# Attention steps in blocks of two, retention outputs turned in pairs, norm factors on weight rows, down's block 6 in seven products

## The chip, the cores and the metric

One core of a Trainium2 chip runs one program. The metric is the device time of one execution in microseconds (us). Smaller is better. The times of before are 1212.03 to 1213.17 us in three runs, median 1212.58.

## What is computed

One layer of a decoder trunk on 512 tokens of width 1024, in float32. `rmsnorm` divides each row by its root mean square and multiplies by a vector of gains.

```python
u = rmsnorm(h, g_pre_mix); proj = u @ w_in          # 1024 -> 12800 columns
yr = rmsnorm(retention(rq, rk, rv)) * silu(rg)      # 4 heads, keys of 256, values of 512
ya = dilated_attention(aq, ak, av)                  # 3 groups of 8 heads of 64, merged by softmax denominators
mixed = sigmoid(gr + b0) * (yr @ w_ret_out) + sigmoid(ga + b1) * (ya @ w_dil_out)
h = h + rmsnorm(mixed @ w_o, g_post_mix)
f = square(relu(rmsnorm(h, g_pre_mlp) @ w_up)) @ w_down   # 1024 -> 4096 -> 1024
h = h + rmsnorm(f, g_post_mlp)
gate = sigmoid(rmsnorm(h, g_pre_ple) @ w_ple_gate + b_ple_gate)
out = h + rmsnorm(gate * (p @ w_ple_in), g_post_ple)
```

In attention's group 0 a query sees up to 256 keys in two blocks of 128 tokens; groups 1 and 2 are cut into streams, and a query block of 128 sees one block of 128 keys.

## The kernel before

**Products.** Each float32 operand is split into a high and a low part, and a product is three passes (`PASSES`: high x high, high x low, low x high). One pass is a TensorE matmul of 128 rows by 128 columns that streams 512 columns; these are the full products (L234, L706, L778, L793, L1030). `acc_tile` does the passes for one token tile of 128 and `gemm` does four tiles, each in a PSUM bank from the pool `pacc` (tiles named a, four banks). All else goes through the pool `pps` (tiles b, four banks).

**Weights.** A weight unit is 256 rows by 512 columns. `plan` and `loads` list all units in order of use. `load_next` starts a load from the SP queue into a token-sized tile (t, pool `pt`, N_T = 26 buffers), and `prep_next` splits one into a tile w (N_W = 5 buffers): ScalarE makes the high part, VectorE the low part. `prep_next` is called when the last token tile has used a unit, so one unit is made for each one consumed.

**Attention as a filler.** Between the products of w_in the kernel does attention in small steps: `filler` spreads a list of steps over the next products, and `pump`, called after each three passes, takes the next when its turn comes. `attention` cuts a group into units: in group 0 four heads of one query block (two units to a block), in groups 1 and 2 all eight. A unit has three steps: `scores` (matmuls over 64 rows, which alternate between the upper and the lower 64 rows and between two banks, then VectorE adds the mask and takes the maximum, and ScalarE takes exponentials), `flip` (TensorE transposes the weights, ScalarE copies them out) and `weigh` (matmuls with the values). The list runs `weigh` of unit i - 2, `flip` of i - 1, `scores` of i. The scheduler of the language then orders the instructions of each engine, by priority and what it takes for ready.

**Retention.** `head` computes one head by a `quartet`. At its end four transposed pieces are put off with `later`, 12, 14, 16 and 18 steps on, each of four transposes into one bank.

**Quartets.** `quartet` computes a product of 2 x 2 blocks with seven block products instead of eight: named "11", 1, "12", 2, 4, 7 and "22", from sums and differences of blocks. The sums of weights are made in `add_quartet`, those of the left operand in `mix_in`, and `result` combines.

**The MLP.** 4096 columns are eight chunks of 512. Chunks 0 to 5 go through `down` in three calls (c = 0 to 2), each a quartet over two chunks, with one `up_unit` (a unit of w_up for a later chunk) behind each block product. Chunks 6 and 7 are plain products with w_down.

**Residuals.** `residual_features` adds a normed row to the residual, multiplies by the next norm's gains (g_pre, on VectorE) and puts the transposes into `vT` or `hT` off by a number of steps (`to_features`, L317). The root mean square itself is applied later.

## Time and profile before

| | |
|---|---|
| median of three runs | 1212.58 us |
| the profiled execution | 1212.39 us |
| its span, first to last instruction | 1210.6 us |
| TensorE (PE) busy | 1196.9 us, 99% |
| weight loads (PEld) busy | 989.3 us, 82% |
| VectorE (DVE) busy | 800.8 us, 66% |
| ScalarE (ACT) busy | 579.1 us, 48% |
| mean granted clock of TensorE | 0.997 |

Times below are from the profiled execution, which took 1.8 us more than its span. In the rows, L with a number is a line of the kernel; names are those of its tiles without numbers; "128x512 f32" is the shape that is read, and x with a number counts the instructions that a row merges. A matmul of a TensorE row is shown with a length of about 0.39 us though the next one starts earlier, so starts are compared, not lengths.

### The profile page before, as it was taken

Reading aid. Unit: us, or ns where it says so; the run is one execution under the profiler, and the core shown is the slowest. Engines: PE = TensorE matmul, PEld = TensorE weight load, DVE = VectorE, ACT = ScalarE, POOL = GpSimd, SP = SyncE. Lnnn points to the kernel's source line nnn. Section 1 sums busy time; section 2 is a strip of 40 time slices with the busy share of each in tenths; the row PEclk is TensorE's granted clock in tenths of the full one; section 3 lists DMA queues with packets and bytes.
Section 4 is the critical chain, followed back from the end, with each engine's and each line's share of the span. In section 5 each row is a group of like instructions: output and inputs, shape, how many; then the busy total and the mean of one; then the engine's idle time right before and its main releaser. Section 6 shows DMA issues by size and latency. Waiting matters only on the chain. (4 is left out here: it accounts for less than half of the span.)

```text
span 1210.6 us, 15131 instructions
## 1 busy us (share of the span) xinstructions
PE 1196.9 (99%) x5646; PEld 989.3 (82%) x5646; DVE 800.8 (66%) x1199; ACT 579.1 (48%) x979; POOL 61.5 (5%) x112
## 2 busy tenths in 40 slices
PE   9999999999999999999999999999999999999996
PEld 7888788888888888888888888888888888888885
DVE  6743644654577895959768467673585775975696
ACT  7334444346744563535445532454553554553362
POOL 1002001000000000000000020020000000000210
PEclk9999999999999999999999999999999999999998
DMA  9432141332241543342335472727142251254401
GB/s 345 143 113 74 41 146 56 115 129 88 88 168 67 198 154 112 131 137 84 127 109 205 137 259 99 289 85 280 36 161 73 82 189 53 87 188 177 156 1 70
DMA packets 53322, 158.87 MB, mean 131 GB/s; under 512 B 8832, under 2 KB 9088, under 8 KB 53248
## 3 DMA queue, kind: packets, MB, share of 16 engines
q1 hardware_dynamic: 39552, 131.82, 30.9%
q10 hardware_dynamic: 9600, 14.53, 3.7%
q0 software_dynamic: 4096, 11.55, 2.6%
q8 instruction: 44, 0.72, 0.2%
q14 instruction: 30, 0.25, 0.1%
HBM read 139.47 MB, written 14.68 MB: 127 GB/s over the span
## 5 line engine op out<-in xcount | busy, mean ns | idle before, releaser
L69 DVE TENSOR_TENSOR w<-t,w 128x1024 fp32r<-128x1024 f32 (+1 forms) x248 | 295.7, 1204 | 144.7 <-ACT w L66 143.4
L66 ACT ACTIVATE w<-t 128x1024 fp32r<-128x1024 f32 (+1 forms) x248 | 256.9, 1044 | 261.9 <-PE a L234 93.7
L234 PE MATMUL a<-u,w 128*128 128x512 f32 x1536 | 369.0, 395 | 1.0 <-ACT t L66 1.0
L234 PEld LDWEIGHTS a<-u,w 128*128 128x128 f32 x1536 | 284.0, 188 | 62.1 <-issue 2.3
L69 DVE TENSOR_TENSOR t<-t,t 128x1024 f32<-128x1024 f32 (+4 forms) x179 | 185.0, 1058 | 26.3 <-ACT t L66 18.5
L706 PE MATMUL b<-w,t 128*128 128x512 f32 x696 | 162.5, 390 | 0.0
L706 PEld LDWEIGHTS b<-w,t 128*128 128x128 f32 x696 | 130.7, 188 | 27.0
L1030 PE MATMUL a<-u,w 128*128 128x512 f32 x576 | 134.0, 390 | 0.0
L1030 PEld LDWEIGHTS a<-u,w 128*128 128x128 f32 x576 | 108.2, 188 | 22.4
L234 PE MATMUL a<-w,u 128*128 128x512 f32 (+1 forms) x504 | 114.3, 384 | 0.2 <-DVE w L69 0.2
L234 PE MATMUL a<-t,w 128*128 128x512 f32 x480 | 110.5, 391 | 0.0
L234 PEld LDWEIGHTS a<-w,u 128*128 128x128 f32 x504 | 91.1, 189 | 18.4 <-DVE w L69 0.5
L69 DVE TENSOR_TENSOR t<-a,t 128x512 f32<-128x512 f32 x72 | 55.7, 776 | 75.3 <-ACT t L66 52.1
L234 PEld LDWEIGHTS a<-t,w 128*128 128x128 f32 x480 | 89.8, 188 | 18.8 <-DVE t L69 0.4
L234 PE MATMUL a<-w,t 128*128 128x512 f32 x432 | 99.6, 391 | 0.0
L234 PEld LDWEIGHTS a<-w,t 128*128 128x128 f32 x432 | 80.8, 188 | 16.7
L66 ACT ACTIVATE t<-t 128x512 fp32r<-128x512 f32 (+1 forms) x55 | 42.1, 787 | 37.7 <-DVE t L69 37.7
L66 ACT ACTIVATE t<-a 80x512 f32<-80x512 f32 (+1 forms) x32 | 18.9, 591 | 69.6 <-PE a L234 64.8
L66 ACT ACTIVATE t<-s 128x256 f32<-128x256 f32 (+3 forms) x94 | 41.8, 488 | 21.2 <-DVE s L69 20.3
L66 ACT ACTIVATE s<-a 128x512 f32<-128x512 f32 x56 | 32.7, 593 | 39.0 <-PE a L234 30.1
L69 DVE TENSOR_TENSOR s<-a,t 128x512 f32<-128x512 f32 x40 | 26.4, 687 | 37.1 <-PE a L234 30.2
L66 ACT ACTIVATE t<-t,st 128x128 f32<-128x128 f32 (+1 forms) x96 | 39.8, 416 | 22.5 <-DVE st L482 19.4
(119 smaller groups left out, 1004.3 us busy)
## 6 DMA issues: line engine op xcount, KB each, us to landing
t<-in_w_in_dram SPq DMA_DIRECT2D x104, 512.0 KB
t<-in_w_down_dram SPq DMA_DIRECT2D x38, 512.0 KB
t<-in_w_up_dram SPq DMA_DIRECT2D x32, 512.0 KB
t<-in_w_ret_out_dram SPq DMA_DIRECT2D x16, 512.0 KB
t<-in_x_dram SPq DMA_DIRECT2D x8, 512.0 KB
yrd<-s ACTq DMA_DIRECT2D x16, 256.0 KB
t<-yrd SPq DMA_DIRECT2D x16, 256.0 KB
t<-in_w_o_dram SPq DMA_DIRECT2D x8, 512.0 KB
```

What stands on the lines that cost most here:

```text
L66: nc.scalar.activation(o, i, f, **kw)
L69: nc.vector.tensor_tensor(o, x, y, op=op)
L234: nc.tensor.matmul(ps, l, r, start=(k == 0 and q == 0), stop=(k == n - 1 and q == 2))
L706: nc.tensor.matmul(ps[t], f(k, i, t), w[:, j, k2], start=(first and k == 0 and n == 0), stop=(k == 3 and n == 2), skip_group_check=not first)
L1030: nc.tensor.matmul(state["ps"][t], w[:, i, k2, t * P:(t + 1) * P], vT[:, x, k], start=(k == 0 and n == 0), stop=(k == 7 and n == 2))
```

## The change

- Attention: units are taken two at a time. A step does `products` of two units, then their `weights` (what was `scores` is cut in these two), or two `flip`s, or two `weigh`s. The number of steps is halved.
- Retention: two transposed pieces are put off together (at 12 and 16), eight transposes in a row into two banks.
- Norm factors: g_pre_mlp and g_pre_ple are no longer multiplied into the residual's rows. They stand in the small tile `cols`, and `divide` multiplies them into the weight rows of w_up and w_ple_gate while it splits these, in two halves. The transposes read the residual itself.
- Buffers: six weight tiles, 24 token-sized tiles.
- The MLP: chunk 6 is also computed by `down`, as a quartet over the halves of one chunk (nk = 1). `gaps` says how many units of w_up follow each block product; the last of the three old calls and the new one have four each.
- In the last down product the additions (`tok_out`) get high priority.

```diff
-N_RAW, N_W, N_T, N_S = 4, 5, 26, 10
+N_RAW, N_W, N_T, N_S = 4, 6, 24, 10
...
+    row_gain = {}
+
+    def divide(w, r, gain):
+        if gain is None:
+            split(w[:, 0], w[:, 1], r)
+            return
+        n, k0 = gain
+        for k in range(2):
+            g = cols[:, n, k0 + k:k0 + k + 1]
+            act(w[:, 0, k], r[:, k], AF.Copy, scale=g)
+            stt(w[:, 1, k], r[:, k], g, w[:, 0, k].bitcast(F32), OP.mult, OP.subtract)
+
...
-        split(w[:, 0], w[:, 1], r)
+        divide(w, r, row_gain.get(ptr["prep"] - 1))
...
-            for k in range(2):
+            for k in range(nk):
...
-            for src, f in between[:1] if name != order[-1] else between:
+            m = gaps[order.index(name)]
+            for src, f, gain in between[:m]:
                 loads.append(src)
+                row_gain[len(plan)] = gain
                 plan.append(f)
-            between = between[1:]
+            between = between[m:]
...
-        add_units(a["w_up"], j)
+        add_units(a["w_up"], j, 3)
+    FULL, SOME = (1, 1, 1, 1, 1, 1, 2), (0, 1, 1, 0, 0, 1, 1)
+
+    def gaps_of(c):
+        return FULL if c + 1 < NC else SOME
+
     for c in range(NC):
-        ups = [(a["w_up"][2 * c + 2 + j, k], pop) for j in range(2) for k in range(4)]
-        add_quartet(lambda kh, nh, k, c=c: a["w_down"][2 * c + kh, nh, k], EARLY, ups)
-    for j in (NFC - 2, NFC - 1):
-        for n in range(2):
-            add_units(a["w_down"][j], n)
+        ups = [(a["w_up"][2 * c + 2 + j, k], pop, (3, 2 * k)) for j in range(2 if c + 1 < NC else 1) for k in range(4)]
+        add_quartet(lambda kh, nh, k, c=c: a["w_down"][2 * c + kh, nh, k], EARLY, ups, 2, gaps_of(c))
+    ups = [(a["w_up"][NFC - 1, k], pop, (3, 2 * k)) for k in range(4)]
+    add_quartet(lambda kh, nh, k: a["w_down"][NFC - 2, nh, kh], EARLY, ups, 1, SOME)
     for n in range(2):
-        add_units(a["w_ple_gate"], n)
+        add_units(a["w_down"][NFC - 1], n)
+    for n in range(2):
+        add_units(a["w_ple_gate"], n, 4)
 
...
-            def scores():
-                sb = [bank(), bank()]
-                sm = got["p"] = big((P, n, w))
-                st = stat(8)
+            def products():
+                sb = got["b"] = [bank(), bank()]
                 for i in range(n):
                     q, hh = divmod(i, 2)
                     rows = slice(hh * 64, hh * 64 + 64)
                     nc.tensor.matmul(sb[hh][:, q * w:(q + 1) * w], at(qT, p0 + q)[rows, t * P:(t + 1) * P],
                                      at(kT, p0 + q)[rows, k0:k0 + w], start=True, stop=True)
+
+            def weights():
+                sb = got["b"]
+                sm = got["p"] = big((P, n, w))
+                st = stat(8)
                 for i in range(n):
                     q, hh = divmod(i, 2)
...
-            return scores, flip, weigh
+            return products, weights, flip, weigh
 
         us = [unit(t, p0) for t in range(NT) for p0 in range(0, 4, pairs)]
+
+        def both(i, parts):
+            def f():
+                for k in parts:
+                    for x in us[2 * i:2 * i + 2]:
+                        x[k]()
+            return f
+
         steps = []
-        for i in range(len(us) + 2):
-            for lag in (2, 1, 0):
-                if 0 <= i - lag < len(us):
-                    steps.append(us[i - lag][lag])
+        m = len(us) // 2
+        for i in range(m + 2):
+            for lag, parts in ((2, (3,)), (1, (2,)), (0, (0, 1))):
+                if 0 <= i - lag < m:
+                    steps.append(both(i - lag, parts))
         return steps
...
-            for kk in range(2):
+            for kk in range(nk):
                 w, = take(1)
...
-                                             start=(first and k == 0 and n == 0), stop=(k == 3 and n == 2),
+                                             start=(first and k == 0 and n == 0), stop=(k == 2 * nk - 1 and n == 2),
...
-        def flip(e):
-            b = bank()
-            for t in range(NT):
-                nc.tensor.transpose(b[:, t * P:(t + 1) * P], sg[t][:, e * P:(e + 1) * P], ident)
-            o = half()
-            act(o, b)
-            nc.scalar.dma_start(yrd[h][e], o)
-
-        for e in range(4):
-            later(12 + 2 * e, lambda e=e: flip(e))
+        def flip(e0):
+            b = {e: bank() for e in (e0, e0 + 1)}
+            for e in b:
+                for t in range(NT):
+                    nc.tensor.transpose(b[e][:, t * P:(t + 1) * P], sg[t][:, e * P:(e + 1) * P], ident)
+            for e in b:
+                o = half()
+                act(o, b[e])
+                nc.scalar.dma_start(yrd[h][e], o)
+
+        for e0 in (0, 2):
+            later(12 + 2 * e0, lambda e0=e0: flip(e0))
...
-    g_pre = bcast(a["g_pre_mlp"])
...
-    def residual_features(t, base, r, gain, rs, dst, rows, lag):
+    def residual_features(t, base, r, rs, dst, rows, lag):
         for n, sl in enumerate(halves):
             with tc.high_priority():
                 stt(base[:, sl], rows[n], r, base[:, sl], OP.mult, OP.add)
-                v = half()
-                tt(v, base[:, sl], gain[:, sl], OP.mult)
-            later(lag, lambda v=v, n=n: to_features(dst, v, t, 4 * n))
+            later(lag, lambda sl=sl, n=n: to_features(dst, base[:, sl], t, 4 * n))
         rstd([sumsq(base[:, sl]) for sl in halves], D, rs)
...
-    def down(c, f0, f1, following):
+    def down(c, quads, following, nk, gaps):
         left = {}
-        a11, a21, a12, a22 = *f0, *f1
+        a11, a21, a12, a22 = quads
...
-                z.append(big((P, 4, 256)))
+                z.append(big((P, 2 * nk, 256)))
...
-        def behind(last):
-            up_unit()
-            if last:
+        def behind(i):
+            for _ in range(gaps[i]):
                 up_unit()
 
-        quartet(EARLY, left, outs, before, dest, behind)
+        quartet(EARLY, left, outs, before, dest, behind, nk)
...
     for c in range(NC):
-        nxt = [quarters() if c + 1 < NC else split_square() for _ in range(2)]
-        down(c, fs[0][0], fs[1][0], nxt)
+        nxt = [quarters() for _ in range(2 if c + 1 < NC else 1)]
+        down(c, [*fs[0][0], *fs[1][0]], nxt, 2, gaps_of(c))
         fs = nxt
-    for n in range(2):
-        gemm(2, list_feed(fs[0][0]), tok_out(facc, n))
+    f = fs[0][0]
+    fs = [None, split_square()]
+    down(NC, [f[0][:, :2], f[1][:, :2], f[0][:, 2:], f[1][:, 2:]], fs[1:], 1, SOME)
     g_post2 = bcast(a["g_post_mlp"])
-    g_pre2 = bcast(a["g_pre_ple"])
...
-            tok_out(facc, n)(t, ps)
+            with tc.high_priority():
+                tok_out(facc, n)(t, ps)
...
-        "cols": np.stack([c.reshape(KT, P).T for c in (v["g_pre_mix"][0], *v["b_gate"][0])], axis=1),
+        "cols": np.stack([c.reshape(KT, P).T for c in (v["g_pre_mix"][0], *v["b_gate"][0], v["g_pre_mlp"][0], v["g_pre_ple"][0])], axis=1),
```

Three places show what becomes of the order. In the rows of the built program, a, b, t, w, u and s are the tiles of the pools above, with the number of each; the shape is that of the result. The first place is TensorE in group 0 of attention, the third query block. Before:

```order
L234 MATMUL a_1096<-u_134,w_872 128x512 x2
L495 MATMUL b_1120<-ident,t_1058 128x128 x2
L234 MATMUL a_1096<-u_134,w_872 128x512
L495 MATMUL b_1120<-ident,t_1058 128x128 x2
L234 MATMUL a_1096<-u_134,w_872 128x512
L495 MATMUL b_1126<-ident,t_1058 128x128 x2
L475 MATMUL b_1146<-t_255,t_253 128x256
L495 MATMUL b_1126<-ident,t_1058 128x128 x2
L475 MATMUL b_1147<-t_255,t_253 128x256
L475 MATMUL b_1146<-t_255,t_253 128x256
L475 MATMUL b_1147<-t_255,t_253 128x256
L234 MATMUL a_1096<-u_134,w_872 128x512 x2
```

Now, at the same block (L495 is the line of `products`, L256 that of `acc_tile`):

```order
L256 MATMUL a_1031<-u_134,w_675 128x512 x6
L256 MATMUL a_1031<-u_134,w_845 128x512 x6
L256 MATMUL a_1031<-u_134,w_856 128x512 x3
L495 MATMUL b_1047<-t_254,t_252 128x256
L495 MATMUL b_1048<-t_254,t_252 128x256
L495 MATMUL b_1047<-t_254,t_252 128x256
L495 MATMUL b_1048<-t_254,t_252 128x256
L495 MATMUL b_1053<-t_255,t_253 128x256
L495 MATMUL b_1054<-t_255,t_253 128x256
L495 MATMUL b_1053<-t_255,t_253 128x256
L495 MATMUL b_1054<-t_255,t_253 128x256
L256 MATMUL a_1031<-u_134,w_856 128x512 x3
```

Transposes (before L495) no longer stand between the scores, and the scores of two units are in one row; before, 24 rows of scores are cut off from each other by other work in the whole program, and now nine.

The second place is TensorE at chunk 6 of the MLP. Before, the first of the plain products (L234; a is one token tile):

```order
L234 MATMUL a_8744<-w_8619,t_8436 128x512 x3
L234 MATMUL a_8744<-w_8619,t_8448 128x512 x3
L234 MATMUL a_8744<-w_8636,t_8460 128x512 x3
L234 MATMUL a_8744<-w_8636,t_8476 128x512 x3
L234 MATMUL a_8758<-w_8619,t_8436 128x512 x3
L234 MATMUL a_8758<-w_8619,t_8448 128x512 x3
L234 MATMUL a_8758<-w_8636,t_8460 128x512 x3
L234 MATMUL a_8758<-w_8636,t_8476 128x512 x3
```

Now block products of the quartet (L740, into banks b) alternate with w_up's units of chunk 7 (L1063):

```order
L1063 MATMUL a_8703<-u_6336,w_8562 128x512 x5
L1063 MATMUL a_8704<-u_6336,w_8562 128x512 x6
L740 MATMUL b_8651<-w_8581,t_8647 128x512 x2
L740 MATMUL b_8651<-w_8581,t_8648 128x512
L740 MATMUL b_8651<-w_8581,t_8647 128x512 x2
L740 MATMUL b_8651<-w_8581,t_8648 128x512
L740 MATMUL b_8652<-w_8581,t_8647 128x512 x2
L740 MATMUL b_8652<-w_8581,t_8648 128x512
L740 MATMUL b_8652<-w_8581,t_8647 128x512 x2
L740 MATMUL b_8652<-w_8581,t_8648 128x512
L1063 MATMUL a_8701<-u_6336,w_8626 128x512 x6
L1063 MATMUL a_8702<-u_6336,w_8626 128x512 x6
```

96 plain products have become 84 products of the quartet. Chunk 7's products with w_up, which stood ahead of chunk 6, now stand between them.

The third place is the end of the first residual, token tiles 2 and 3, on TensorE. Before (s is the row multiplied by the gains):

```order
L234 MATMUL a_6633<-w_6328,t_6175 128x512 x3
L234 MATMUL a_6633<-w_6328,t_6178 128x512 x3
L317 MATMUL b_6645<-ident,s_6498 128x128 x4
L317 MATMUL b_6652<-ident,s_6501 128x128 x4
L317 MATMUL b_6689<-ident,s_6586 128x128 x4
L317 MATMUL b_6696<-ident,s_6589 128x128 x4
L234 MATMUL a_6662<-w_6522,t_6175 128x512 x3
L234 MATMUL a_6662<-w_6522,t_6178 128x512 x3
```

Now the transposes read the residual's tile t itself:

```order
L256 MATMUL a_6621<-w_6326,t_6175 128x512 x3
L256 MATMUL a_6621<-w_6326,t_6178 128x512 x3
L339 MATMUL b_6635<-ident,t_6169 128x128 x4
L339 MATMUL b_6642<-ident,t_6169 128x128 x4
L256 MATMUL a_6652<-w_6508,t_6175 128x512 x3
L256 MATMUL a_6652<-w_6508,t_6178 128x512 x3
L256 MATMUL a_6662<-w_6508,t_6175 128x512 x3
L256 MATMUL a_6662<-w_6508,t_6178 128x512 x3
L256 MATMUL a_6672<-w_6508,t_6175 128x512 x3
L256 MATMUL a_6672<-w_6508,t_6178 128x512 x3
L339 MATMUL b_6679<-ident,t_6171 128x128 x4
L339 MATMUL b_6686<-ident,t_6171 128x128 x4
```

The sixteen transposes in one row are two rows of eight with 18 products between them. On VectorE, token tile 3, before:

```order
L69 TENSOR_TENSOR u_6338<-b_6560,u_6338 128x4x128
L294 SCALAR_TENSOR_TENSOR t_6171<-s_6336,st_6583,t_6171 128x512
L294 SCALAR_TENSOR_TENSOR t_6171<-s_6577,st_6583,t_6171 128x512
L69 TENSOR_TENSOR s_6586<-t_6171,t_6183 128x512
L69 TENSOR_TENSOR s_6589<-t_6171,t_6183 128x512
L69 TENSOR_TENSOR u_6338<-b_6567,u_6338 128x4x128
L69 TENSOR_TENSOR w_6640<-t_6536,w_6640 128x1024
```

and now:

```order
L69 TENSOR_TENSOR u_6336<-b_6552,u_6336 128x4x128
L325 TENSOR_SCALAR st_6573<-st_6571 128x1
L69 TENSOR_TENSOR u_6336<-b_6559,u_6336 128x4x128
L316 SCALAR_TENSOR_TENSOR t_6171<-s_6334,st_6575,t_6171 128x512
L316 SCALAR_TENSOR_TENSOR t_6171<-s_6569,st_6575,t_6171 128x512
L316 SCALAR_TENSOR_TENSOR w_6628<-t_6524,cols,w_6628 128x512 x2
```

The two products with the gains (s from t and t) are gone, and the split of a weight tile is two operations with `cols`.

## Rows read from the trace of the kernel before

**Rows 1.** The page, busy time of each engine, share of the span, instructions.

```profile
PE 1196.9 (99%) x5646; PEld 989.3 (82%) x5646; DVE 800.8 (66%) x1199; ACT 579.1 (48%) x979; POOL 61.5 (5%) x112
```

**Rows 2.** Windows, every engine, 850 to 1100 us: length, then busy us (instructions).

```profile
850.00:1100.00 250.00, 250.00 (x1105) 207.19 (x1104) 176.59 (x177) 123.20 (x162) 1.11 (x2) 1.00 0.32 115
```

**Rows 3.** Windows of attention: full products (L234), transposes (L495), weighing (L506).

```profile
83.17:336.26 253.09, 203.33 (x820) 150.42 (x820) 1.00 0.27 88
83.17:336.26 253.09, 20.95 (x120) 14.81 (x120) 1.00 0.27 88
83.17:336.26 253.09, 28.48 (x240) 29.24 (x240) 1.00 0.27 88
```

**Rows 4.** Timeline of TensorE in group 1: start, length in us, line, shapes.

```profile
198.36 5.06 PE L234 MATMUL a<-u,w 128*128 128x512 f32 x21
...
204.96 5.06 PE L234 MATMUL a<-u,w 128*128 128x512 f32 x21
...
210.65 5.02 PE L234 MATMUL a<-u,w 128*128 128x512 f32 x21
215.59 1.16 PE L475 MATMUL b<-t,t 64*128 64x128 f32 x16
216.69 5.06 PE L234 MATMUL a<-u,w 128*128 128x512 f32 x21
```

**Rows 5.** Timeline of TensorE, first scores of group 1.

```profile
185.58 0.73 PE L234 MATMUL a<-w,u 128*128 128x512 f32 x2
...
186.89 4.61 PE L234 MATMUL a<-w,u 128*128 128x512 f32 x19
```

**Rows 6.** Timeline of TensorE, 256-wide scores of group 0 between products.

```profile
96.98 3.00 PE L234 MATMUL a<-w,u 128*128 128x512 f32 x12
...
100.97 2.33 PE L234 MATMUL a<-u,w 128*128 128x512 f32 x9
```

**Rows 7.** Timeline of TensorE, retention outputs of head 0, four transposes between products.

```profile
463.34 1.64 PE L234 MATMUL a<-u,w 128*128 128x512 f32 x6
...
465.17 1.64 PE L234 MATMUL a<-u,w 128*128 128x512 f32 x6
```

**Rows 8.** Groups by form, ScalarE and VectorE: count, busy us, mean ns, idle before.

```profile
L66 ACT ACTIVATE t<-t,st 128x128 f32<-128x128 f32 x72 | 27.9, 390 | 14.5 <-DVE st L482 14.5
L66 ACT ACTIVATE w<-t 128x1024 fp32r<-128x1024 f32 x240 | 251.9, 1058 | 260.7 <-PE a L234 93.7 <-PE b L706 57.7 <-PE a L1030 46.8
L66 ACT ACTIVATE u<-t,cols 128x512 fp32r<-128x512 f32 x8 | 5.8, 724 | 3.1 <-DMA t<-in_xT_dram 2.0 <-DMA cols<-in_cols_dram 0.9
L69 DVE TENSOR_TENSOR w<-t,w 128x1024 fp32r<-128x1024 f32 x240 | 290.2, 1221 | 143.7 <-ACT w L66 142.5
L294 DVE SCALAR_TENSOR_TENSOR u<-t,cols,u 128x512 fp32r<-128x512 f32 x8 | 6.0, 752 | 5.1 <-ACT u L66 4.9
L69 DVE TENSOR_TENSOR s<-t,t 128x512 f32<-128x512 f32 x16 | 10.3, 686 | 0.0
L479 DVE CUSTOM_DVE_ANT_0 t<-b,masks 128x256 f32<-128x256 f32 x24 | 9.0, 420 | 9.0 <-PE b L475 8.9
```

**Rows 9.** Windows, every engine, 1050 to 1150 us.

```profile
1050.00:1150.00 100.00, 100.00 (x447) 82.98 (x446) 69.95 (x95) 40.89 (x58) 8.56 (x15) 1.00 0.47 163
```

**Rows 10.** Timeline of TensorE, transposes after the first residual.

```profile
806.25 5.71 PE L234 MATMUL a<-w,t 128*128 128x512 f32 x24
...
814.25 0.66 PE L317 MATMUL b<-ident,s 128*128 128x128 f32 x4 [0.48 <-DVE u L69]
814.81 3.47 PE L234 MATMUL a<-w,t 128*128 128x512 f32 x14
```

**Rows 11.** Timeline of TensorE, transposes after the second residual, third token tile.

```profile
1154.36 3.79 PE L234 MATMUL a<-w,u 128*128 128x512 f32 x16
1158.52 1.23 PE L317 MATMUL b<-ident,s 128*128 128x128 f32 x8 [0.37 <-DVE s L69]
1159.50 8.22 PE L234 MATMUL a<-w,u 128*128 128x512 f32 x35
```

More of the change, by code (lines that the diff above doesn't have):

```diff
@@ L118, in prep_next, with add_units, add_quartet @@
             load_next()
-    def add_units(w, n):
+    def add_units(w, n, gain=None):
         for kk in range(w.shape[1]):
             loads.append(w[n, kk])
+            if gain is not None:
+                row_gain[len(plan)] = (gain, 2 * kk)
             plan.append(pop)
     EARLY, LATE = ("11", 1, "12", 2, 4, 7, "22"), ("11", 1, 2, 4, 7, "12", "22")
-    def add_quartet(quarter, order, between=()):
+    def add_quartet(quarter, order, between=(), nk=2, gaps=(1, 1, 1, 1, 1, 1, 2)):
         x, y, z, v = {}, {}, {}, {}
@@ L256, in gemm @@
             evac(t, ps)
-    cols = const.tile([P, 3, KT], F32, name="cols")
+    cols = const.tile([P, 5, KT], F32, name="cols")
     nc.scalar.dma_start(cols, a["cols"])
@@ L656, in left_sums, with quartet @@
         quads["22"] = lambda k, x, t: u[:, x, 4 + k, (2 + t) * P:(3 + t) * P]
-    def quartet(order, left, outs, before={}, dest={}, behind=None):
+    def quartet(order, left, outs, before={}, dest={}, behind=None, nk=2):
         pa, pb, pc, p1, q, u2 = ({} for _ in range(6))
@@ L719, in quartet @@
             if behind:
-                behind(name == order[-1])
+                behind(order.index(name))
     def rope_pair(x1, x2):
@@ L940, in wo_second @@
             r = rstd([ssq[t], s], D)
-        residual_features(t, h1[t], r, g_pre, rs1[:, t:t + 1], vT, (r0[t], z), 16 if t < 3 else 14)
+        residual_features(t, h1[t], r, rs1[:, t:t + 1], vT, (r0[t], z), 16 if t < 3 else 14)
         nc.gpsimd.dma_start(h1d[t], h1[t])
@@ L1001, in mix_in @@
             src = {"11": a11, "12": a12, 7: a21, "22": a22}.get(name) if name not in (1, 2, 4) else z[0]
-            o = [big((P, 4, 256), F32R) for _ in range(2)]
+            o = [big((P, 2 * nk, 256), F32R) for _ in range(2)]
             split(o[0], o[1], src)
@@ L1076, in hybrid_block @@
             tt(r, r, rs1q[:, t:t + 1], OP.mult)
-        residual_features(t, h1[t], r, g_pre2, rs2[:, t:t + 1], hT, [part(t, n) for n in range(2)], 12)
+        residual_features(t, h1[t], r, rs2[:, t:t + 1], hT, [part(t, n) for n in range(2)], 12)
     e = {n: pair_tiles() for n in range(2)}
@@ L1185 @@
     }
-    for n in ("g_post_mix", "g_pre_mlp", "g_post_mlp", "g_pre_ple", "g_post_ple"):
+    for n in ("g_post_mix", "g_post_mlp", "g_post_ple"):
         ins[n] = v[n]
```

## Prediction

> **What bounds the kernel now.** I read the page first. TensorE is busy in 1196.9 of 1210.6 us [rows 1], so the end moves only when TensorE gets less to do, does it faster, or waits less. Busy time on a pipelined engine hides how fast it runs, so the next view is a stretch with full products alone: 250.0 us hold 1105 of them [rows 2], two of which began before it, which gives 250.0 / 1103 = 0.2267 us for one 128x512 product (p below) at a granted clock of 1.00, the 2.4 GHz level. VectorE is busy in 176.6 of these 250.0 us and ScalarE in 123.2: they have room there.
>
> The one long stretch in which TensorE is slower than p is attention. From 83.17 to 336.26, 253.09 us, it does 820 full products [rows 3]; one of them began before, so 819 x 0.2267 = 185.7 us, and 67.4 us go to small work: 240 records of weighing values, 120 transposes, and the scores. The steady part of group 1 shows what a run of each kind takes [rows 4]: from the start of one run of full products to the start of the next, less the 21 products in it (4.76 us), a run of 16 weighing records (left out between the first two rows) takes 6.60 - 4.76 = 1.84, a run of eight transposes (left out too) 5.69 - 4.76 = 0.93, a run of 16 score records 6.04 - 4.76 = 1.28. (A score or weighing matmul in float32 leaves two records, a transpose one.) By these rates weighing is 240 x 0.115 = 27.6 us, transposing 120 x 0.116 = 13.9, and the scores get the other 25.9.
>
> **The change, part by part.** Scores in blocks of two steps. Two runs of eight score records with two products between them [rows 5]: the second takes 1.31 - 2p = 0.86. Two of these would be 1.72, but one run of 16 takes 1.28. So a run pays 0.44 for being entered and left, and each eight records 0.42. The 256-wide scores of group 0 take 3.99 - 12p = 1.27 for eight records [rows 6], that is 0.44 and 0.83; no run of 16 of these is in the trace, so this split is an estimate. In the built order the change has nine score runs instead of 24: two of eight (0.86 each), three of 16 that are 256 wide (0.44 + 1.66 = 2.10), four of 32 that are 128 wide (0.44 + 4 x 0.42 = 2.12). That is 1.7 + 6.3 + 8.5 = 16.5 us, 9.4 less than 25.9. Fifteen entries are 6.6 of it. The other 2.8 I put down to group 0, where the old order sometimes puts transposes or products between two score matmuls that alternate between banks; the new order leaves them together. Bounds: if the wide runs gained nothing by their length, they would be 3 x 2 x 1.27 = 7.6, and the gain 8.1; if transposes and weighing also gain by longer runs, 10.2.
>
> Retention outputs in pairs: four transposes take 1.83 - 6p = 0.47 [rows 7], eight take 0.93 [rows 4], so a merged pair saves 0.01 and the eight pairs 0.1. I take 0.1; bounds 0 and 0.4 (hundredths of reading).
>
> Block 6 in seven products: two calls of 48 products (96) become seven of 12 (84), 12p = 2.7 us less on TensorE. The price is on the others. VectorE gets three more weight splits and four sums of weight tiles (7 x 1.22 [rows 8] = 8.5), 11 half-size operations for the left operands and ten for combining results, less eight for squares (13 x about 0.69 = 9.0): 17.5 us more. From 1050 to 1150 it is busy in 70.0 of 100 us [rows 9], so it would be 87.5 of 97: TensorE still covers it, with little left for order.
>
> Norm factors on weight rows: 16 VectorE products of 0.686 go (11.0 us), and with each half the chain from residual to transposes gets 0.686 shorter. Each of the 40 weight tiles is prepared in two halves: ScalarE 2 x 0.724 - 1.058 = 0.39 more, VectorE 2 x 0.752 - 1.221 = 0.28 more [rows 8], 15.6 and 11.3 us over some 340. Full products hide both: six products per tile and token tile. Two loads of gains go as well. I cost this at nothing on the path, but it takes waits away. At 806 to 815 sixteen transposes take 8.56 - 24p = 3.12 [rows 10], 1.26 more than two runs of eight, with a wait of 0.48 for VectorE at the last four. The new order puts 18 products between token tiles 2 and 3, and the transposes read the residual itself. At 1158 a run of eight takes 5.14 - 16p = 1.51 [rows 11], 0.58 more than its 0.93. There the transposes of tile 2 come four products (0.9 us) earlier than now, but one operation of 0.686 leaves the chain in front of them and two the queue of the tile before; moreover the additions of the tile go ahead by priority. I take both waits as gone: 1.8. Bounds 0.6 (only the first, by half) and 1.9.
>
> What the change adds in waits: the paired step gives ScalarE 16 exponentials in one row, 16 x 0.39 = 6.2 us [rows 8], instead of eight, 3.1. Behind them in its queue stand the splits of the next weight tiles, 1.06 each on ScalarE and then 1.22 on VectorE, and TensorE waits for these. Six weight tiles instead of five put one more prepared tile in front, six products = 1.36 us of cover. A burst that falls just as a matrix product changes its weights can be bare for 3.1 - 1.4 = 1.7 us less what slack there was. There are eight bursts, and most fall inside a product, not at its end; I take 0.9 us in all, with bounds 0 and 5. The token pool falls from 26 tiles to 24; the loads that it limits are 4 deep as before, and TensorE waits for no load in any row above, so nothing is put down for it.
>
> Sum: 9.4 + 0.1 + 2.7 + 1.8 - 0.9 = 13.1 us. The profiled execution took 1212.39, 0.2 below the median of the three runs, so the two can stand for each other: **1199.3**.
>
> **The rivals.** *Banks hold TensorE up.* A paired step fills all four rotating PSUM banks; the next step, 21 products (4.76 us) later in group 0, needs one back. VectorE's eight reductions take 8 x 0.375 = 3.0 us (9.0 us for 24 [rows 8]). With one weight split ahead of them it is 4.2, with two 5.4: then 0.7 late. At about nine of the steps that would be 6.3 us: 1205.6. Against it: groups 1 and 2 have 42 products between steps, twice the time. The Trainium skill (TensorEngine Tiling (Array Packing), PSUM Bottleneck) speaks for this rival and against the change: cutting the array into tiles, as the 64-row scores do, speeds up TensorE, it says, but not the evacuation of PSUM, which may become the bottleneck. No row of before shows such a wait in attention.
>
> *The entry price is not shared*: if scores paid per group of eight records, nothing would come of the blocks, and the time would be 1212.4 - 2.7 - 1.8 - 0.1 + 0.9 = 1208.7. Rows 5 against rows 4 speak against it.
>
> *ScalarE's bursts decide* (slower): if each burst's extra lay bare, 3.1 at the four of groups 1 and 2 and 4 x 0.39 = 1.6 at the four of group 0, TensorE would wait 18.7 us where I put down 0.9, and the time would be 1199.3 + 17.8 = 1217.1. It turns to slower than before when three quarters of it lie bare (14 of 18.7). Against it are the sixth weight tile, and that a matrix product asks for new weight tiles only at its start, while most of a burst falls inside it.
>
> **How the numbers follow.** Forecast 0.67 (its own range 1196.5 to 1203: the upper bounds of scores and pairs, 10.2 and 0.4, with no new wait, give 1197.2, and 0.02 us of reading error on some 30 runs a little less; 8.1 for scores and 2.5 us of new waits give 1202). Banks 0.17, entry price not shared 0.08, bursts 0.05, of which 0.04 end slower and 0.01 about even; 0.03 for no change by things unseen. The range 1196.5 to 1205.7 holds the first two. Less than 0.2% (2.4 us) is about what a measurement here can't tell from no change; so faster 0.92, same 0.04, slower 0.04.
>
> **What would show it.** In attention nine score runs, of 16 or 32 records, at 2.1 us each, and the stretch from first score to last weighing 9 to 10 us shorter for equal products. Block 6 with 84 products, VectorE near 88% around it and no TensorE wait over half a microsecond. No wait before the transposes at the two residuals. The forecast is wrong if score runs of 32 take over 3 us, or if TensorE's waits on ScalarE or VectorE in attention add up to more than 3 us.

## The result and the profile after

The changed kernel takes 1198.32 us (1197.71 to 1198.64, four runs) against 1212.43 (1212.03 to 1213.17) of before on the same chip: 0.988 of it, with a 95% interval of 0.9865 to 0.9896. Spans are 1196.3 and 1210.6 us, so 14.3 us went. The forecast was 1199.3, faster, with a range from 1196.5 to 1205.7.

The page of the changed kernel, busy times, beside [rows 1]:

```profile
PE 1183.7 (99%) x5634; PEld 985.7 (82%) x5634; DVE 813.7 (68%) x1243; ACT 588.5 (49%) x1031; POOL 65.3 (5%) x112
```

TensorE is still the bound, so the 14.3 us must be found in its own row. The window from the first score to the last weighing, full products, beside [rows 3]:

```profile
85.76:327.25 241.49, 191.28 (x808) 149.46 (x808) 1.00 0.30 98
```

One of the 808 products began before the window. 241.49 - 807 x 0.2267 = 58.5 us go to the small work, 8.9 less than the 67.4 of before, at the same granted clock of 1.00. Twelve products that stood in this stretch now stand ahead of it, so the stretch got 11.6 shorter.

TensorE's timeline shows score rows of a block, 256 wide in group 0 and 128 wide in group 1, and two rows of retention transposes; they answer to [rows 4 to 7]:

```profile
113.18 5.05 PE L256 MATMUL a<-u,w 128*128 128x512 f32 x21
118.16 2.00 PE L495 MATMUL b<-t,t 64*128 64x256 f32 x16
120.08 5.10 PE L256 MATMUL a<-u,w 128*128 128x512 f32 x21
...
197.40 9.79 PE L256 MATMUL a<-u,w 128*128 128x512 f32 x42
207.12 2.06 PE L495 MATMUL b<-t,t 64*128 64x128 f32 x32
209.11 9.82 PE L256 MATMUL a<-u,w 128*128 128x512 f32 x42
...
454.57 2.98 PE L256 MATMUL a<-u,w 128*128 128x512 f32 x12
457.39 1.03 PE L849 MATMUL b<-ident,s 128*128 128x128 f32 x8
458.18 4.11 PE L256 MATMUL a<-u,w 128*128 128x512 f32 x17
```

Read as in the prediction: 6.90 - 21p = 2.14 us for 16 wide score records (256 columns), 11.71 - 42p = 2.19 for 32 narrow ones (128 columns), 3.61 - 12p = 0.89 for eight transposes. Below I give such lengths more finely, from the start of the last product ahead of a row to that of the sixth behind it, less six products: 2.17, 2.21 and 0.893. These take the pipeline's edges in and repeat within 0.01 or 0.02 from row to row. The order holds nine score rows: two of 0.87, three of 2.17, four of 2.21, 17.1 us in all. By the same reading the scores of before took about 26.1 (where they share a row with transposes, at the price of these).

Starts of single records, which the merged rows above don't show, tell what happens inside such a row. In the changed kernel's score rows the records start in pairs, some 0.006 us apart: 16 pairs in each row of 32, one every 0.11 us, and eight in each row of 16, one every 0.21. In before the rows of [rows 4] have their pairs too, but in group 0 eight pieces of two or four records stand without any.

The timeline at the two residuals, beside [rows 10, 11]:

```profile
796.37 5.70 PE L256 MATMUL a<-w,t 128*128 128x512 f32 x24
801.92 1.03 PE L339 MATMUL b<-ident,t 128*128 128x128 f32 x8
802.75 4.38 PE L256 MATMUL a<-w,t 128*128 128x512 f32 x18
806.97 1.04 PE L339 MATMUL b<-ident,t 128*128 128x128 f32 x8
...
1144.40 5.70 PE L256 MATMUL a<-w,u 128*128 128x512 f32 x24
1149.94 1.03 PE L339 MATMUL b<-ident,t 128*128 128x128 f32 x8
1150.73 4.57 PE L256 MATMUL a<-w,u 128*128 128x512 f32 x19
```

No row stands with a wait. All eight rows of transposes together take 7.23 us; before, the seven rows took 9.32.

The window over block 6 and the second residual, every engine, beside [rows 9], and then TensorE's waits in the whole program (waiting line, what released it: us in total, times, longest):

```profile
1040.00:1140.00 100.00, 100.00 (x449) 82.15 (x448) 86.85 (x128) 52.44 (x88) 9.55 (x17) 1.00 0.47 169
```

```profile
PE b L290 <- DVE s L287: 1.5, 1, 1.5
PE a L256 <- ACT t L66: 0.7, 1, 0.7
PE a L256 <- ACT w L66: 0.5, 1, 0.5
PE a L256 <- DVE w L69: 0.2, 1, 0.2
```

VectorE went from 70 to 87 us in 100, as put down, and TensorE waits for it nowhere there. The only wait that the change brings is the third, 0.5 us in attention. The trace holds 4788 full products, 12 fewer. The account of the span:

| term, us saved | predicted | measured |
|---|---|---|
| attention, scores less new waits | 9.4 - 0.9 = 8.5 | 8.9 |
| block 6, twelve products | 2.7 | 2.7 |
| transposes at the two residuals | 1.8 | 2.1 |
| retention pairs | 0.1 | 0.4 |
| first 32 us | 0 | 0.3 |
| sum | 13.1 | 14.4 |

The spans differ by 14.3; the last tenth is reading. Attention's 8.9 are 9.0 on the scores and 0.2 on the weighing, which now stands in longer rows, less 0.3 on the transposes and the new wait.

### The profile page after: what moved, and what is told of

The parts are those of the page before. It is cut to its first block, busy times and chain, and to the rows that moved or that the text cites. A ratio compares the mean times of both kernels' runs of the same rounds, so it can differ in the third digit from the quotient of the medians.

```text
span 1196.3 us, 15173 instructions
## 1 busy us (share of the span) xinstructions
PE 1183.7 (99%) x5634; PEld 985.7 (82%) x5634; DVE 813.7 (68%) x1243; ACT 588.5 (49%) x1031; POOL 65.3 (5%) x112
## 4 chain that ended last, share of the span: by engine, by line
PE 97%; ACT 1%; DVE 1%; DMA 1%; SPq 0%; issue 0%; ACTq 0%; DVEq 0%; POOLq 0%
PE a L256 53%; PE b L740 17%; PE a L1063 11%; PE a L740 7%; PE b L827 2%; PE b L531 2%; PE b L812 1%; PE b L495 1%; PE b L520 1%; ACT t L66 1%; PE b L339 1%; PE b L849 1%; DMA t<-in_w_in_dram 1%; DVE t L316 0%; DVE t L504 0%; PE b L623 0%
## 5 line engine op out<-in xcount | busy, mean ns | idle before, releaser
L256 PE MATMUL a<-u,w 128*128 128x512 f32 x1536 | 358.7, 392 | 1.2 <-ACT t L66 0.7
L256 PEld LDWEIGHTS a<-u,w 128*128 128x128 f32 x1536 | 285.7, 188 | 61.5 <-issue 1.0
L66 ACT ACTIVATE w<-t 128x1024 fp32r<-128x1024 f32 (+1 forms) x211 | 217.7, 1042 | 209.4 <-PE a L256 71.6
L69 DVE TENSOR_TENSOR w<-t,w 128x1024 fp32r<-128x1024 f32 (+1 forms) x211 | 251.4, 1200 | 95.1 <-ACT w L66 93.4
L69 DVE TENSOR_TENSOR t<-t,t 128x1024 f32<-128x1024 f32 (+4 forms) x193 | 196.6, 1043 | 32.5 <-ACT t L66 18.1
L740 PE MATMUL b<-w,t 128*128 128x512 f32 x780 | 182.7, 390 | 0.0
L740 PEld LDWEIGHTS b<-w,t 128*128 128x128 f32 x780 | 146.1, 188 | 31.2 <-ACT t L66 0.7
L1063 PE MATMUL a<-u,w 128*128 128x512 f32 x576 | 134.8, 389 | 0.0
L1063 PEld LDWEIGHTS a<-u,w 128*128 128x128 f32 x576 | 108.1, 188 | 22.5
L256 PE MATMUL a<-w,u 128*128 128x512 f32 (+1 forms) x504 | 113.2, 383 | 0.2 <-DVE w L69 0.2
L256 PE MATMUL a<-t,w 128*128 128x512 f32 x480 | 109.7, 390 | 0.0
L256 PEld LDWEIGHTS a<-w,u 128*128 128x128 f32 x504 | 91.3, 189 | 18.8 <-DVE w L69 0.5
L256 PEld LDWEIGHTS a<-t,w 128*128 128x128 f32 x480 | 89.9, 188 | 18.6
L316 DVE SCALAR_TENSOR_TENSOR w<-t,cols,w 128x512 fp32r<-128x512 f32 x80 | 57.5, 747 | 45.4 <-ACT w L66 45.3
L256 PE MATMUL a<-w,t 128*128 128x512 f32 x336 | 78.3, 392 | 0.0
L256 PEld LDWEIGHTS a<-w,t 128*128 128x128 f32 x336 | 62.4, 188 | 13.2 <-DVE t L69 0.3
L66 ACT ACTIVATE w<-t,cols 128x512 fp32r<-128x512 f32 x80 | 53.9, 716 | 38.4 <-PE a L1063 27.2
```

Of the source, the lines that this page charges most:

```text
L66: nc.scalar.activation(o, i, f, **kw)
L69: nc.vector.tensor_tensor(o, x, y, op=op)
L256: nc.tensor.matmul(ps, l, r, start=(k == 0 and q == 0), stop=(k == n - 1 and q == 2))
L316: return nc.vector.scalar_tensor_tensor(o, x, s, y, op0=op0, op1=op1)
L740: nc.tensor.matmul(ps[t], f(k, i, t), w[:, j, k2], start=(first and k == 0 and n == 0), stop=(k == 2 * nk - 1 and n == 2), skip_group_chec ...
L1063: nc.tensor.matmul(state["ps"][t], w[:, i, k2, t * P:(t + 1) * P], vT[:, x, k], start=(k == 0 and n == 0), stop=(k == 7 and n == 2))
```

## The experiments

Each kernel below ran beside the kernel before; its median is given with the ratio to that. The changed kernel itself gave 1198.32 at first and 1198.86 (1197.86 to 1199.46; 0.9884, 0.9869 to 0.9899) beside the last kernels, as after_again. So a difference of under 1 us between kernels that did not run side by side says nothing, and I read the small terms from the traces.

**Which part carries it: no_blocks and blocks_only.** The first is the changed kernel with attention's old list of steps:

```diff
...
-                if 0 <= i - lag < m:
-                    steps.append(both(i - lag, parts))
+                if 0 <= i - lag < len(us):
+                    steps.append(single(us[i - lag], lag))
```

> The changed kernel with attention's steps one unit at a time again, all else as changed. Theory (a score run pays 0.44 us for being entered and left, and scores that alternate between the halves lose when other work stands between them): the built order has 23 score runs instead of 9, 14 x 0.44 = 6.2 us, and about 2 us for the broken alternation in group 0; a wait of about 0.6 us on ScalarE in attention goes. 1198.3 + 6.2 + 2 - 0.6 = 1206. Rival (the price is paid per group of eight score records, shared or not; the gain came from products and waits alone): 1198.3. Rival (the blocks' gain is less small work in between of any kind): transposes and weighing would be dearer per record than 0.11 us, scores not.

The second is the kernel before with the new attention alone (`products`, `weights`, `both`).

> The kernel before with only attention's blocks of two. Theory: the stretch from the first score to the last weighing loses what it lost in the changed kernel, about 9 us: 1212.4 - 8.9 = 1203.5, with 9 score runs; the five weight tiles make ScalarE's burst of exponentials show by 0.5 us more at most. Rival (blocks pay only together with six weight tiles): waits on the weight splits in attention of several us, 1206 or more. Rival (price not shared): 1212.

no_blocks: 1207.25 us (0.9957, 0.9942 to 0.9972); small work in attention 67.0 us, with one wait of 0.71 for VectorE ahead of a score row. blocks_only: 1204.57 (0.9928, 0.9911 to 0.9944); 58.4 us, and with five weight tiles no wait in attention is listed: the blocks don't need the sixth. The blocks are worth 8.3 to 8.9 us whether added alone or taken away last, and the parts add up: 8.3 and the 5.6 that no_blocks keeps, against 14.1. In no_blocks' trace, in the old order of group 0, one unit's scores are cut in two pieces of four records. TensorE's timeline:

```profile
120.75 3.01 PE L256 MATMUL a<-u,w 128*128 128x512 f32 x12
123.69 1.13 PE L495 MATMUL b<-t,t 64*128 64x256 f32 x4
124.75 3.24 PE L256 MATMUL a<-u,w 128*128 128x512 f32 x13
127.92 1.13 PE L495 MATMUL b<-t,t 64*128 64x256 f32 x4
```

The first piece takes 4.00 - 12p = 1.28 us, as much as all eight records of a unit that stand together (1.27 as read in [rows 6], 1.29 by the finer reading). A second entry explains 0.4 of this and no more. Its four records start 0.22 us apart or more, none in pairs.

**What an entry costs: scores_apart.** The scores of a block's two units are put in two steps with products between, the rest stays in pairs:

```diff
-                    steps.append(both(i - lag, parts))
...
+                        steps.append(first[0])
+                        steps.append(lambda x=first, y=second: (y[0](), x[1](), y[1]()))
```

> The changed kernel, in which the scores of the second unit of a block are a step of their own; transposes, weighing, maxima and exponentials stay in blocks of two, and no score run is broken by transposes. 16 score runs instead of 9. Theory (entry price): 7 x 0.44 = 3.1 us more, 1201.4; each run of 8 (128 wide) 0.86, of 16 1.3 us. Rival (only the broken alternation in group 0 cost, not the entry): 1198.3. Rival (what blocks save is in transposes and weighing): 1198.3 too, but then no_blocks is slow and this is not.

1200.72 us (0.9901, 0.9887 to 0.9916). 16 score rows, for instance:

```profile
199.69 7.74 PE L256 MATMUL a<-u,w 128*128 128x512 f32 x33
207.36 1.16 PE L495 MATMUL b<-t,t 64*128 64x128 f32 x16
208.45 7.10 PE L256 MATMUL a<-u,w 128*128 128x512 f32 x30
```

By the finer reading a row of 16 narrow records takes 1.316 and one of eight wide records 1.287. With 0.869 for eight narrow and 2.21 for 32, the narrow rows lie on one line: 0.422 + 0.0559 a record. The wide ones give 0.40 + 0.1105 a record. Seven more entries are 2.9 us; the small work in attention grew by 2.0, because the wait of 0.5 us and a cut in the transposes beside it, 0.85 together, went away. The burst of 16 exponentials did not. ScalarE has them in one row still, but with four weight splits ahead of it, of which the last is shown:

```profile
190.68 1.05 ACT L66 ACTIVATE w<-t 128x1024 fp32r<-128x1024 f32 x1
192.87 0.40 ACT L66 ACTIVATE t<-t,st 128x128 f32<-128x128 f32 x1 [1.13 <-DVE st L507]
```

Small work that uses all 128 rows pays no such price. Rows of 8, 16 and 32 weighing records take 0.915 to 0.919, 1.808 and 3.595 us, rows of 4, 8 and 16 transposes 0.47, 0.893 and 1.77. So the rival of no_blocks, that any small work in between is dear, is out.

**Do the halves work together: halves_in_turn and halves_by_block.** The prediction said of group 0 only that score matmuls "alternate between banks". In halves_in_turn a unit's upper halves come first, then its lower halves:

```diff
-                for i in range(n):
+                for i in [*range(0, n, 2), *range(1, n, 2)]:
```

> The changed kernel with the scores of a unit ordered by half: first all heads on the upper 64 rows, then all on the lower. Same 9 runs, same records. Theory (two scores on different halves run at once, so that the 2.8 us beside the entries was lost where they did not follow each other): the part of the runs beyond their entry, about 17.1 - 9 x 0.44 = 13 us, nearly doubles: 1198.3 + 13 = 1211, runs of 32 at 0.44 + 3.4 = 3.9 us. Rival (each score takes its time whatever is beside it, and the rest of the old loss was waits): 1198.3.

1201.69 us (0.991, 0.9895 to 0.9925), attention 3.1 us longer: a real cost, but far from a doubling. The timeline of group 1's second block:

```profile
198.38 9.80 PE L256 MATMUL a<-u,w 128*128 128x512 f32 x42
208.11 2.82 PE L495 MATMUL b<-t,t 64*128 64x128 f32 x32
210.86 7.36 PE L256 MATMUL a<-u,w 128*128 128x512 f32 x31
```

This row takes 2.99 by the finer reading, 0.78 more than alternating. The wide rows, where a half has only four records in turn, rise from 2.17 to 2.25. My theory as it stood, that only neighbours in strict alternation overlap, fell. I formed another: TensorE starts a record of the other half while it is at work on the first, but looks only some three records ahead; nine of 32 records overlap at three changes of half. The starts bear this out: such a row has nine pairs. halves_by_block leaves one change in a row:

```diff
...
-                    for x in us[2 * i:2 * i + 2]:
-                        x[k]()
+                    for half in range(1 if k else 2):
+                        for x in us[2 * i:2 * i + 2]:
+                            x[k](*([half] if k == 0 else []))
```

> The scores of a block come in four rows of matmuls: the upper halves of both units, then the lower halves, so that a half follows itself 8 times (16 records of 128 columns, 8 of 256) where the changed kernel alternates at each matmul. Theory (the two halves of the array work at the same time, but TensorE looks ahead only some three records past the one it works on, as a run of 32 with halves in turn at 2.99 us against 2.21 gives: nine of 32 records overlap at three changes of half): only three records overlap at the one change, so a run of 32 takes 0.42 + 29 x 0.112 = 3.66 us and a run of 16 that is 256 wide 0.40 + 13 x 0.221 = 3.28; with 4 x 1.45 + 3 x 1.11 = 9.1 us more than the changed kernel the time is near 1207.4. Rival (a price per change of half, 0.26 us, and no overlap): with one change instead of three or of fifteen the runs get no longer than 2.47, and the time is 1199 to 1200.

1208.69 us (0.9963, 0.9951 to 0.9976). The timeline, a wide and a narrow row:

```profile
116.96 5.05 PE L256 MATMUL a<-u,w 128*128 128x512 f32 x21
121.94 2.96 PE L497 MATMUL b<-t,t 64*128 64x256 f32 x16
124.84 5.10 PE L256 MATMUL a<-u,w 128*128 128x512 f32 x21
...
202.30 11.40 PE L256 MATMUL a<-u,w 128*128 128x512 f32 x49
213.63 3.50 PE L497 MATMUL b<-t,t 64*128 64x128 f32 x32
217.06 1.19 PE L256 MATMUL a<-u,w 128*128 128x512 f32 x4
```

The narrow rows take 3.64 (3.66 expected), the wide ones 3.14 (3.28), and attention 8.6 us more than the changed kernel's. The rival, a price per change of half, is out: fewer changes cost more. The starts show the overlap itself: a row of 32 has three pairs. A record as long as a row's first, 0.373 us, comes a second time right after the thirteenth start, three records before the first half's sixteen are through; in the wide rows it comes after the fifth of eight. The median is 1.2 us more than attention's 8.6 above after_again. In the profiled execution, itself 1.1 above the median, the first score comes 2.3 us later than in the changed kernel (the start, below); where the median's 1.2 lie is not shown.

In all these kernels the upper halves' scores also go to one bank and the lower halves' to another. No run separates the two, so what part the banks have in the overlap stays open.

**Block 6: no_seven.** Chunk 6 as plain products again:

```diff
...
-    down(NC, [f[0][:, :2], f[1][:, :2], f[0][:, 2:], f[1][:, 2:]], fs[1:], 1, SOME)
+    for n in range(2):
+        gemm(2, list_feed(fs[0][0]), tok_out(facc, n))
```

(The list of weight units goes back with it.)

> The changed kernel with chunk 6 as plain products again, all else as changed. Theory (12 products less, and VectorE's 17.5 us more lie beside products): 12 x 0.2267 = 2.7 us more, 1201.0, VectorE near 70% in the last 150 us. Rival (VectorE's load made TensorE wait and ate part of it): 1199 to 1200.

1200.87 us (0.9901, 0.9884 to 0.9919), 4800 products, 2.0 to 2.6 above the changed kernel's two medians for 2.7 of products. No new wait stands around the chunk in either. VectorE is busy for 798.9 us here and for 813.7 in the changed kernel, so the quartet costs it 14.8 us, where the prediction had 17.5.

**Norm factors: gains_on_tokens.** The gains are multiplied into the residual's rows again:

```diff
...
+                v = half()
+                tt(v, base[:, sl], gain[:, sl], OP.mult)
-            later(lag, lambda sl=sl, n=n: to_features(dst, base[:, sl], t, 4 * n))
+            later(lag, lambda v=v, n=n: to_features(dst, v, t, 4 * n))
```

> The changed kernel with the norm gains multiplied into the residual's rows on VectorE again (two loads and 16 products more), and plain splits of the weights. Theory (the shorter chain took the waits before the transposes away): 1.2 us before the last transposes of the first residual and 0.6 at the second come back, 1198.3 + 1.8 = 1200.1. Rival (the waits went by the other order and the priority of the additions, not by the shorter chain): 1198.3 to 1198.8, no wait of more than 0.3 us at the transposes.

1201.52 us (0.9905, 0.989 to 0.9921). TensorE's timeline after the first residual:

```profile
802.82 2.06 PE L339 MATMUL b<-ident,s 128*128 128x128 f32 x16
805.84 5.73 PE L256 MATMUL a<-w,t 128*128 128x512 f32 x24 [0.95 <-ACT s L66]
```

The sixteen transposes stand together again and TensorE waits behind them. All transposes at the residuals take 9.14 us, 1.9 more than now, close to the 9.32 of before. VectorE is busy for 85.5 of the 100 us from 1040, no more than now (86.9), and around the first residual for 26.7 of the 50 us from 780, where it is 24.8 now. So the gain is the shorter chain and the order that comes with it, which this run does not separate, and not relief for VectorE. The median is 2.7 above after_again's; of what is left beside 1.9, the profile shows a first score that comes 0.9 us later.

**The burst and its cover: weights_apart and five_tiles.** In weights_apart the second unit's `weights` get a step of their own in groups 1 and 2, so that ScalarE has eight exponentials in a row there:

```diff
...
+                        steps.append(lambda x=first, y=second: (x[0](), y[0](), x[1]()))
+                        steps.append(second[1])
```

> The changed kernel; in groups 1 and 2 maxima and exponentials of the block's second unit are a step of their own, so that ScalarE gets two bursts of eight and not one of 16; score runs stay in blocks of two. Theory (the one wait for a weight split in attention, 0.5 to 0.7 us, comes from the burst of 16): it goes, 1197.7. Rival (the wait has another cause, as the transposes' copies or loads): it stays, 1198.3.

1198.17 us (0.988, 0.9864 to 0.9895). The wait in attention is gone and attention is 0.8 us shorter, but the time can't be told from the changed kernel's. Here too splits stand ahead of the second eight, four of them. So with scores_apart the wait hangs on the splits that are due right behind the burst, more than on the burst's length. Five_tiles gives the buffers back:

```diff
-N_RAW, N_W, N_T, N_S = 4, 6, 24, 10
+N_RAW, N_W, N_T, N_S = 4, 5, 26, 10
```

> The changed kernel with five weight tiles and 26 token tiles as before. Theory (the sixth tile covers 1.36 us of a late split): the wait on weight splits in attention grows by up to 1.4 us, 1198.3 to 1199.7. Rival (the sixth tile covers nothing that is late): 1198.3 within 0.3.

1200.41 us (0.99, 0.9885 to 0.9916), but attention takes 241.3 us, not longer. The wait behind the burst is even shorter than with six tiles, 0.15 us for 0.51 (and again 0.15 in five_again):

```profile
195.20 12.77 PE L256 MATMUL a<-u,w 128*128 128x512 f32 x55 [0.15 <-ACT w L66]
```

Since the extra could have been chance, I ran it once more beside the changed kernel.

> The changed kernel with five weight tiles and 26 token-sized ones, once more. Its first median was 2.1 us above the changed kernel's, measured in another call, while its attention took 241.3 us as there. Theory (the difference is of the first loads, by chance): the medians differ by less than 1 us in one call. Rival (the sixth tile is worth 2 us at the start): again 1.5 to 2.5 us above after_again, and its trace shows where.

> The changed kernel itself, once more, beside the others. The waits of its first 32 us (0.23 and 0.70 us in the first profile, 0.5 to 3.2 in other kernels that are the same there) are put down to when the first loads land; by this they come out otherwise in a second execution, by up to 1 us, while attention from the first scores to the last weighing stays at 241.5 us to within 0.1. Time 1197.5 to 1199.5. Rival (they belong to the kernel's layout): 0.23 and 0.70 us again.

1200.29 us (0.9897, 0.9882 to 0.9912) against 1198.86, 1.4 us that lie between the theory and the rival, with intervals that overlap; so the traces have to tell. Five_again's timeline at the second residual shows where time is lost:

```profile
1144.61 2.75 PE L256 MATMUL a<-w,u 128*128 128x512 f32 x11
1147.59 0.98 PE L256 MATMUL a<-w,u 128*128 128x512 f32 x3 [0.23 <-DVE w L316]
1148.85 2.56 PE L256 MATMUL a<-w,u 128*128 128x512 f32 x10 [0.29 <-DVE w L316]
1151.26 1.03 PE L339 MATMUL b<-ident,t 128*128 128x128 f32 x8
```

24 products take 6.65 us instead of 5.54, in both profiles with five tiles and in none with six: VectorE's split of w_ple_gate with the gains (L316) comes late. The sixth tile is worth 1.1 us, there. (The token-sized tiles went from 24 back to 26 with it, which was not tried apart; the rows wait for a weight split.)

The waits of the first 32 us do change by chance. Five_tiles and five_again are one kernel, and beside the first 1.49 us they wait 2.4 and 1.1 us there. After_again's timeline:

```profile
8.83 0.50 PE L256 MATMUL a<-w,u 128*128 128x512 f32 x1 [0.23 <-ACT w L66]
9.55 19.15 PE L256 MATMUL a<-w,u 128*128 128x512 f32 x83 [0.22 <-DVE w L69]
29.61 43.83 PE L256 MATMUL a<-u,w 128*128 128x512 f32 x192 [0.47 <-ACT t L66]
```

In the changed kernel's first profile the first of these is missing and the last is 0.70, so the sum is 0.9 both times, put otherwise, while attention came out the same to 0.02 us. In halves_by_block the first is 2.39, in no_blocks 1.99 (ScalarE waits there 3.10 us for a load of w_in). So up to 1 or 2 us of a single run is the start.

**Retention: no_pairs.** Four transposes at a time again:

```diff
...
-        for e0 in (0, 2):
-            later(12 + 2 * e0, lambda e0=e0: flip(e0))
+        for e in range(4):
+            later(12 + 2 * e, lambda e=e: flip(e))
```

> The changed kernel with the retention outputs transposed four at a time again (16 rows of four instead of eight rows of eight). By the prediction's term 0.1 us more than the changed kernel; by the rows of four in the trace of before, 0.467 each against 0.893 for eight, 8 x 0.041 = 0.33 us more. Both lie within what a measurement tells; the lengths of the rows in the trace decide: 0.47 for four, and no wait. A rival, that the gaps between the rows hide a wait for ScalarE's copies, would show TensorE waiting there.

1199.31 us (0.989, 0.9875 to 0.9904). Sixteen rows of four at 0.46 to 0.47 us, 7.5 in all, against 8 x 0.893 = 7.15: 0.4 us, and no wait.

## Why the prediction was right

**Scores.** Predicted 9.4, measured 9.0. The two steps behind it both hold. Fifteen entries at 0.44 were put at 6.6; an entry costs 0.40 to 0.42, so 6.2. The other 2.8 were "put down to group 0", as a remainder, and a remainder of 2.8 is what is left. Its cause was named only by half: the scores of the upper and the lower 64 rows work at the same time, and a cut that leaves matmuls of one half in a piece takes their partners away. The eight pieces of before without pairs are all in group 0. The units cut there lack twelve wide pairs, 0.22 us each, and two narrow ones, 0.11 each, and these are the 2.8. A cut unit pays 1.28 + 1.26 = 2.54 instead of 1.29, of which 0.4 is the entry and 0.85 the lost overlap. Halves_by_block shows that overlap by itself. The Trainium skill (TensorEngine Tiling (Array Packing), Key Properties) says that a change of the tiling mode drains TensorE, and that tiles work independently; the entry of 0.40 to 0.42 and the lost 0.85 agree with it. That tiles work independently holds here only for records that are issued near each other, as 2.99 and 3.64 us for a row of 32 show beside 2.21.

**New waits.** Predicted 0.9, measured 0.5, with 0.85 lost around it in all; a split behind the burst came late, as the mechanism has it, at one burst of eight. TensorE, ScalarE and then VectorE, first block of group 1:

```profile
194.39 0.73 PE L256 MATMUL a<-u,w 128*128 128x512 f32 x2 [0.51 <-ACT w L66]
```

```profile
192.91 0.39 ACT L66 ACTIVATE t<-t,st 128x128 f32<-128x128 f32 x1
193.20 0.19 ACT L66 ACTIVATION_READ_ACCUMULATOR t<-t,st 128x1 f32 x1
193.29 1.04 ACT L66 ACTIVATE w<-t 128x1024 fp32r<-128x1024 f32 x1
```

```profile
194.37 3.50 DVE L69 TENSOR_TENSOR w<-t,w 128x1024 fp32r<-128x1024 f32 x3 [6.19 <-ACT w L66]
```

The last exponential is followed at once by the split that was due, VectorE had waited 6.19 us for it, and TensorE 0.51. The step that was wrong here is the cover: the sixth tile was to take 1.36 us off this wait, and with five tiles the wait is 0.15 and not 0.51. The sixth shields the second residual (1.1 us), where the prediction put no price on it; so the term came out near 0.9 partly by luck. By scores_apart and weights_apart the wait goes where splits stand ahead of the burst; why it is shorter with five tiles is not shown.

**Residuals.** Predicted 1.8 with 1.9 as the upper bound, measured 2.1, so the bound was too low; 0.1 of it is the last row of before, cut in two at 1167 us, which the prediction left out. No wait is left, as said. **Block 6** came out at its twelve products. **Retention** was under-sized: two readings that were good to hundredths (0.47 and 0.93) hid a difference of 0.045 a pair; by the finer reading eight take 0.893.

**The sum.** Predicted 13.1, measured 14.4, with terms that erred both ways: scores 0.4 too high; waits 0.6 too dear, since 0.85 is lost around the one wait but transposes that before were cut up gain 0.5 elsewhere; residuals and retention 0.3 too low each. The weighing's 0.2 and the start's 0.3 had no term; the second is chance. The stretch became 8.9 us shorter for equal products, a little under the 9 to 10 that it named as a sign.

**The rivals.** *Banks*: no wait for a reduction in attention, with 42 products between the blocks or with 21. The remark of the Trainium skill on the evacuation of PSUM (TensorEngine Tiling (Array Packing), PSUM Bottleneck) is made for a fourfold speed-up, where the scores here run on two halves; no run shows such a wait, and it decides nothing here. *Entry price not shared*: rows of 32 would take 3.5, not 2.21. *Bursts*: 0.5 of the 18.7 us that could have lain bare, and not by the sixth tile's merit: with five it is 0.15.

## What to carry to other kernels

Put matmuls over 64 rows in one long row and alternate the halves within it (here each half had a bank of its own): every return to 128 rows costs some 0.4 us, and a piece that holds one half alone takes as long as one with both. Before a buffer is credited to one place, look at every place where its engine is nearly full; the one that pays may be 900 us away. Judge terms of a few tenths from rows of the trace, since the first loads alone move a run by 1 us.

## What was not expected

TensorE overlaps the two halves without strict alternation, as long as few records of one half follow each other: four in a row cost 0.08 us in a row of 16, eight in a row 0.78 in a row of 32, sixteen in a row 1.43. These fit an overlap of three records at each change of half, and the starts of the narrow rows show it, three pairs at each change; that this is a queue of that length is only argued. Why the load of w_in lands so differently at the start was not tried.
